# A two-layer decoder step: the third feed-forward layer's gate and up as Strassen products, and the state-space preparation moved beside the second

## Chip, core and metric

The kernel runs on one core of one Trainium2 chip. The metric is the device time of one execution in microseconds. PE is TensorE (matrix products), DVE is VectorE, ACT is ScalarE, POOL is GpSimd, and SP is the engine that issues most loads.

## What is computed

Two decoder layers run on 512 prompt tokens and 8 sample tokens, which the kernel keeps together as 520 columns. Each layer has a gated feed-forward layer, a mixer, a cross-attention and a second gated feed-forward layer. The mixer is a gated MLP in layer 0 and a diagonal state-space model in layer 1:

```python
def _swiglu(h, wg, wu, wd):
    return (jax.nn.silu(h @ wg) * (h @ wu)) @ wd
...
    for i in range(DEPTH):
        x = x + 0.5 * _swiglu(_rmsnorm(x, norm_ffn1[i]), ffn1_wg[i], ffn1_wu[i], ffn1_wd[i])
        ...
        x = x + out                                # mixer
        x = x + _cross_attn(...)
        x = x + 0.5 * _swiglu(_rmsnorm(x, norm_ffn2[i]), ffn2_wg[i], ffn2_wu[i], ffn2_wd[i])
    return _rmsnorm(x, norm_final), ...
```

The width is 1024, the hidden width 2816, everything in float32. So there are four feed-forward layers in time order: "first" (layer 0, before the mixer), "second" (layer 0, after it), "third" (layer 1, before the mixer) and "fourth". The state-space mixer needs tables made from its weights alone (powers of the diagonal times B and C, a convolution kernel, cosines and sines). This is the preparation that the change moves; it depends on nothing that the trunk computes.

## The kernel before

Activations lie transposed: 8 tiles of 128 features by 520 columns, in two halves of 260. A float32 product is made of three matmuls of rounded parts: weight-high times x-high, weight-high times x-low, weight-low times x-high. `wsplit` makes the parts: ACT rounds the raw weight `wr` into `wh` (line 121), and DVE, or POOL for every fourth weight (`pool_every`), subtracts to give `wl` (line 124). Each of `wr`, `wh` and `wl` has four buffers, and PSUM four tiles.

`ffn` (line 407) runs blocks of 256 hidden columns, 11 in all. `gu(j)` makes gate and up of one block with four calls of `lin`, 48 matmuls of 128x128 by 260 columns each, so 192. `down(a, b)` then takes hidden tiles a to b (128 columns each) through the down projection: 8 output tiles with 6(b−a) matmuls each, and DVE adds each output tile to X (lines 524 and 292 make the residual and the next layer's scaled input `xs`). Which hidden tiles go together is set by `FFN_GROUPS = ((0,6),(6,12),(12,18),(18,22))`. One `gu` beyond the group is always made ahead of its `down`, since line 558 runs `gu` up to `g1 // 2 + 1`.

The fourth layer has `seven=True`. Its first two blocks (`PLAIN = 2`) are plain; blocks 2 to 10 go through `gu7`, which makes each 2x2 block product (two halves of the inner dimension, 128-column halves of the weights, column halves of x) with seven products of 24 matmuls in place of eight, so 168. The price is sums: of x halves once per layer (`seven_x`, `xb` and `xt`, line 309), of weight quarters per block on POOL (`seven_begin`, line 348) and DVE, and of PSUM results on DVE. It uses `SEVEN_GROUPS`, in steps of four hidden tiles and a last one of two.

The state-space preparation `s5_prep` (line 1056) is a generator. `fill()` at the end of each `gu` and of each `down` but the last takes one more step of it. Before, the second and third layers both carry steps, and the rest is drained behind the third. In it POOL makes the powers in 128x128 pieces (`cmul`, lines 1214 to 1226), POOL and DVE make the phases (lines 1254 to 1264), PE turns and multiplies small tiles (line 80), and DVE copies them out (lines 1272 to 1293).

A layer's norm is applied late. DVE sums the squares of X (lines 235 and 236, POOL part of them), PE multiplies the sum with ones (`ones,sq`), DVE takes the inverse root, and the scale `rs` multiplies the first PSUM results. A scheduler places each engine's instructions in one fixed order when the program is built, and each engine runs its row in order.

Of the kernel before, what the change touches and what calls it, by code (L numbers as in the profile page):

```python
# [42 lines left out]
class Prog:  # L43
# [362 lines left out]

    def ffn(self, l, pre, fill=lambda: None, start=False, finish=None, seven=False):
        nc, ins = self.nc, self.ins
# [38 lines left out]
        def gu(j):  # L447
# [14 lines left out]
            for m in range(2):  # L462
# [15 lines left out]
                self.split(s, w)  # L478
                hid[2 * j + m] = s
            fill()  # L480

# [74 lines left out]
        done = 0  # L556
        for g0, g1 in SEVEN_GROUPS if seven else FFN_GROUPS:
            while done < min(DFF // 256, g1 // 2 + 1):
                (gu7 if seven and done >= PLAIN else gu)(done)
                done += 1  # L560
                if seven and done == 1:
                    ops, more = self.seven_x(key, xs)
                    late.append(more)
            if g1 == DFF // 128 and finish:
                last(g0, g1)
            else:
                down(g0, g1)
# [488 lines left out]
    def s5_prep(self):  # L1056
# [67 lines left out]
        nc.scalar.activation(s2, r, AF.Sin, scale=TP / 2)  # L1124
        pw = self.const([128, 5, 2, NPAIR], "pw")
        self.pw = pw
# [3 lines left out]
        V.tensor_sub(nr, em1, t)  # L1130
        V.tensor_scalar(pw[:, 1, 0], nr, 1.0, None, op0=ALU.add)
        V.tensor_mul(pw[:, 1, 1], mag, s1)
        ni = pw[:, 1, 1]
        den, a, b = f(), f(), f()
# [12 lines left out]
        V.tensor_mul(fim, a, den)  # L1147
        for j in range(2, 5):
            V.tensor_mul(a, pw[:, j - 1, 0], pw[:, 1, 0])
            V.tensor_mul(b, pw[:, j - 1, 1], pw[:, 1, 1])  # L1150
            V.tensor_sub(pw[:, j, 0], a, b)
            V.tensor_mul(a, pw[:, j - 1, 0], pw[:, 1, 1])
            V.tensor_mul(b, pw[:, j - 1, 1], pw[:, 1, 0])
            V.tensor_add(pw[:, j, 1], a, b)
# [51 lines left out]
        self.s5d = []  # L1206
        HQ = 8
        for hf in range(4):
            q0 = hf * HQ
            yield  # L1210
            MB, ME = (self.slot([128, 2, HQ, 4, 16], F32, "M") for _ in range(2))
            MB, ME = ([x[:, c] for c in range(2)] for x in (MB, ME))

            def cmul(dst, src, j, neg):
                ar, ai = bc16(pw[:, j, 0], q0, q0 + HQ), bc16(pw[:, j, 1], q0, q0 + HQ)
                xr, xi = src[:, 0, q0 : q0 + HQ], src[:, 1, q0 : q0 + HQ]
                a, b = (self.tmp([128, HQ, 16], tag="t") for _ in range(2))
                G.tensor_mul(a, xr, ar)
                G.tensor_mul(b, xi, ai)
                G.tensor_sub(dst[0], a, b)  # L1220
                a, b = (self.tmp([128, HQ, 16], tag="t") for _ in range(2))
                G.tensor_mul(a, xr, ai)
                G.tensor_mul(b, xi, ar)
                G.tensor_add(dst[1], a, b)
                if neg:
                    G.tensor_scalar(dst[1], dst[1], -1.0, None, op0=ALU.mult)

            for tau in range(4):
                if tau == 3:
                    for c in range(2):  # L1230
                        G.tensor_copy(MB[c][:, :, 3], Bb[:, c, q0 : q0 + HQ])
                else:
                    cmul([MB[c][:, :, tau] for c in range(2)], Bb, 3 - tau, False)
                cmul([ME[c][:, :, tau] for c in range(2)], CT, tau + 1, True)
            for i in range(2 * hf, 2 * hf + 2):
# [7 lines left out]
                for c in range(2):  # L1243
                    for g in range(2):
                        hp = slice(64 * g, 64 * g + 64)
                        nc.scalar.copy(Bs[hp, c, :, :, g], MB[c][hp, l0 : l0 + 4])
                        nc.scalar.copy(Es[hp, c, :, :, g], ME[c][hp, l0 : l0 + 4])
                        nc.scalar.activation(Cm[hp, c, :, g], CT[hp, c, 4 * i : 4 * i + 4], AF.Copy,
                                             scale=-1.0 if c else 1.0)
# [45 lines left out]
                for n, src, w in (("bi", bi, 1024), ("es", Es, 1024), ("tb", tb, 1024), ("tt", Tt, 512)):  # L1295
# [4 lines left out]
                    dd.append(d)  # L1300
                self.s5d.append(dd)

    def s5(self, fill=lambda: None):
# [85 lines left out]
        def emit(i, vv, H):  # L1389
# [4 lines left out]
            for t in range(4):  # L1394
                for j, (w, m) in enumerate(((Tt, vv), (Es[:, 0], H[0]), (Es[:, 1], H[1]))):
                    for a in range(4):
                        self.mm(p[32 * a : 32 * a + 32, t // 2, (t % 2) * 136 : (t % 2) * 136 + 136],
                                w[:, a, 32 * t : 32 * t + 32], m[:, a, 0:136], j == 0, j == 2)
            z = self.tmp()
# [22 lines left out]
        for i in range(KT):  # L1422
# [12 lines left out]
            prev = vv, H  # L1435
        ab = [self.pw[:, 1, c].unsqueeze(2).to_broadcast([128, NPAIR, NB]) for c in range(2)]
        h1 = []
# [122 lines left out]
    def run(self):  # L1560
# [7 lines left out]
        def drain(gen):  # L1568
            for _ in gen:
                pass  # L1570
# [11 lines left out]
        prep = self.s5_prep()  # L1582
        self.ffn(0, False, steps(prep))
        self.tap("ffn2_0")
        self.ffn(1, True, steps(prep))
        drain(prep)
        self.tap("ffn1_1")
# [36 lines left out]
```

## Time and profile before

| | us |
|---|---|
| median of 3 runs | 2456.07 |
| lowest, highest run | 2452.64, 2461.69 |
| the profiled execution's own time | 2454.6 |
| its span (first to last instruction) | 2452.9 |

The page names PE as the busiest engine, with 97% of the span. The windows view gives for a stretch the busy time of each engine, the clock that PE was granted (1.00 is the level of 2.4 GHz, 0.50 that of 1.2 GHz) and the load of the DMA engines. The timeline gives one row per instruction or run of equal instructions: start, duration, engine, line, operation, and in brackets the idle time ahead of it and who ended it. In the stretch from 912 to 1703 us stand the second layer (to 1306) and the third; the state-space mixer begins at about 1703 us and the fourth layer at 2072 us.

### The profile page before, as it was taken

How to read it: one execution, taken by the hardware profiler on the slowest of the kernel's cores; microseconds unless marked ns; L12 is line 12 of the kernel's file. 1: busy time of each engine (PE TensorE's matmuls, PEld its weight loads, DVE VectorE, ACT ScalarE, POOL GpSimd, SP SyncE). 2: the span in 40 equal slices, each digit the busy share in tenths (PEclk: the TensorE clock that was granted, in tenths of full speed). 3: DMA queues.
4: the chain of work that ended last, by engine and by line, in shares of the span. 5: the costliest groups of instructions: out<-in, count | busy, mean ns of one | idle time of the engine just before them, and what ended most of it. 6: DMA issues, size and time to landing. Idle time of an engine off the chain costs nothing. (4 is left out here: it accounts for less than half of the span.)

```text
span 2452.9 us, 46675 instructions
## 1 busy us (share of the span) xinstructions
PE 2386.8 (97%) x19943; PEld 2312.7 (94%) x19943; DVE 1456.5 (59%) x2500; ACT 849.0 (35%) x1312; POOL 526.5 (21%) x511
## 2 busy tenths in 40 slices
PE   8999999999999999999999999999989999999998
PEld 7999999999999789999999999998769979999998
DVE  6534343648556646545557555545993564788885
ACT  4323222432323333233234323323423333544443
POOL 2101111102112011262522625211040101122221
PEclk8999999999999999999999999999999999999998
DMA  6243433322224632324234343323752562133331
GB/s 191 86 139 108 151 97 94 113 88 62 87 87 160 226 130 79 117 79 142 82 117 134 100 134 104 121 87 129 265 183 92 174 228 98 52 104 93 98 104 53
DMA packets 235662, 293.34 MB, mean 120 GB/s; under 512 B 7423, under 2 KB 203767, under 8 KB 235455
## 3 DMA queue, kind: packets, MB, share of 16 engines
q1 hardware_dynamic: 222247, 254.88, 32.2%
q10 hardware_dynamic: 12567, 34.38, 4.0%
q8 instruction: 157, 2.57, 0.4%
q0 software_dynamic: 640, 1.10, 0.2%
q14 instruction: 51, 0.41, 0.1%
HBM read 264.77 MB, written 25.56 MB: 118 GB/s over the span
## 5 line engine op out<-in xcount | busy, mean ns | idle before, releaser
L77 PE MATMUL ps<-xs,wh 128*128 128x260 f32 x6592 | 1082.7, 284 | 3.9 <-ACT xs L291 2.5
L77 PEld LDWEIGHTS ps<-xs,wh 128*128 128x128 f32 x6592 | 918.6, 189 | 7.9 <-ACT xs L291 3.0
L77 PE MATMUL ps<-xs,wl 128*128 128x260 f32 x3296 | 689.4, 283 | 0.3 <-POOL wl L124 0.3
L121 ACT ACTIVATE wh<-wr 128x1024 fp32r<-128x1024 f32 (+2 forms) x388 | 353.5, 913 | 940.0 <-PE ps L77 846.1
L77 PEld LDWEIGHTS ps<-xs,wl 128*128 128x128 f32 x3296 | 520.7, 189 | 0.6 <-POOL wl L124 0.6
L124 POOL TENSOR_TENSOR wl<-wr,wh 128x1024 fp32r<-128x1024 f32 (+2 forms) x94 | 196.5, 2091 | 1349.1 <-ACT wh L121 1334.0
L77 PE MATMUL ps<-hid,wh 128*128 128x260 f32 (+1 forms) x2816 | 456.0, 283 | 2.8 <-ACT hid L161 1.8
L77 PEld LDWEIGHTS ps<-hid,wh 128*128 128x128 f32 x2816 | 388.4, 189 | 4.7 <-ACT hid L161 2.3
L124 DVE TENSOR_TENSOR wl<-wr,wh 128x1024 fp32r<-128x1024 f32 (+2 forms) x294 | 326.8, 1113 | 84.3 <-ACT wh L121 83.5
L77 PE MATMUL ps<-hid,wl 128*128 128x260 f32 (+2 forms) x1408 | 286.3, 283 | 0.0
L77 PEld LDWEIGHTS ps<-hid,wl 128*128 128x128 f32 x1408 | 218.2, 189 | 0.0
L524 DVE SCALAR_TENSOR_TENSOR X<-ps,X 128x520 f32<-128x520 f32 x136 | 94.7, 696 | 179.9 <-PE ps L77 179.6
L475 DVE TENSOR_TENSOR t<-ps,rs 128x520 f32<-128x520 f32 x70 | 48.8, 697 | 183.5 <-PE ps L77 182.5
L473 DVE TENSOR_TENSOR t<-ps,rs 128x520 f32<-128x520 f32 x70 | 48.8, 697 | 137.9 <-PE ps L77 105.6
L162 DVE TENSOR_TENSOR hid<-t,hid 128x520 fp32r<-128x520 f32 x88 | 87.1, 990 | 27.5 <-ACT hid L161 26.5
L161 ACT ACTIVATE hid<-t 128x520 fp32r<-128x520 f32 x88 | 56.2, 638 | 114.9 <-DVE t L476 110.2
L77 PE MATMUL ps<-o,wh 128*128 128x260 f32 x512 | 92.5, 291 | 1.2 <-DVE o L162 0.7
L77 PE MATMUL ps<-z,wh 128*128 128x260 f32 x512 | 83.3, 284 | 1.9 <-ACT t L1402 1.0
L77 PE MATMUL ps<-um,wh 128*128 128x260 f32 x512 | 82.5, 283 | 0.0
L77 PE MATMUL ps<-xt,wh 128*128 128x260 f32 x432 | 79.9, 285 | 1.6 <-ACT wh L344 1.6
L77 PEld LDWEIGHTS ps<-o,wh 128*128 128x128 f32 x512 | 74.5, 188 | 6.5 <-issue 3.0
L235 POOL TENSOR_TENSOR sq<-sq,sq 128x520 f32<-128x520 f32 x22 | 32.8, 1492 | 217.4 <-ACT sq L231 216.8
(352 smaller groups left out, 2946.0 us busy)
## 6 DMA issues: line engine op xcount, KB each, us to landing
wr<-in_ffn_wg SPq DMA_DIRECT2D x34, 1024.0 KB, 5.4
wr<-in_ffn_wu SPq DMA_DIRECT2D x34, 1024.0 KB, 5.4
wr<-in_ffn_wd SPq DMA_DIRECT2D x36, 768.0 KB, 4.7
wr<-in_ffn_wd SPq DMA_DIRECT2D x32, 512.0 KB, 3.5
wr<-in_a_w_in SPq DMA_DIRECT2D x16, 1024.0 KB, 5.5
kc<-in_cache_mem_k SPq DMA_DIRECT2D x32, 512.0 KB, 7.4
vc<-in_cache_mem_v SPq DMA_DIRECT2D x32, 512.0 KB, 7.6
wr<-in_ffn_wg SPq DMA_DIRECT2D x20, 512.0 KB, 3.9
```

What stands on the lines that cost most here:

```text
L77: self.nc.tensor.matmul(out, lhsT=lhsT, rhs=rhs, start=start, stop=stop, **kw)
L121: nc.scalar.activation(hi, r, AF.Copy)
L124: eng.tensor_sub(lo, r, hi.bitcast(F32))
L161: nc.scalar.activation(sl[:, 0, n0:n1], src, AF.Copy)
L162: nc.vector.tensor_sub(sl[:, 1, n0:n1], src, sl.bitcast(F32)[:, 0, n0:n1])
L235: (nc.gpsimd if k == 7 and early or k < 4 and not early else nc.vector).tensor_add(sums[-1], sums[-1], t)
L473: nc.vector.tensor_mul(self.v2(t), pg[:, :, :HN], rs)
L475: nc.vector.tensor_mul(self.v2(w), pu[:, :, :HN], rs)
L524: nc.vector.scalar_tensor_tensor(xv, p[:, :, :HN], 0.5, xv, op0=ALU.mult, op1=ALU.add)
```

## The change

The third layer is called with `seven=True` and without `fill`. The second layer is called with `fine=True`: it keeps the plain `gu`, takes two steps of the preparation in each `gu` instead of one, and uses `SEVEN_GROUPS`. While it runs `pool_every` is so large that no weight is split on POOL, and the preparation is drained at its end. `cmul` becomes `powers`, which makes three or four powers in one instruction on POOL (384 or 512 elements a row); a sign moves into ACT's copy (line 1246 of the kernel after), and the mixer reads the `es` table in the reversed order of powers.

```diff
-    def ffn(self, l, pre, fill=lambda: None, start=False, finish=None, seven=False):
+    def ffn(self, l, pre, fill=lambda: None, start=False, finish=None, seven=False, fine=False):
...
                 hid[2 * j + m] = s
+                if fine and m == 0:
+                    fill()
             fill()
...
-        for g0, g1 in SEVEN_GROUPS if seven else FFN_GROUPS:
+        for g0, g1 in SEVEN_GROUPS if seven or fine else FFN_GROUPS:
...
+        def powers(src, q0, i0):
+
+            M = self.slot([128, 2, HQ, 4, 16], F32, "M")
+            n = 4 - i0
+            sh = [128, HQ, n, 16]
+            ar, ai = (pw[:, i0:4, c, q0 : q0 + HQ].rearrange("p t q -> p q t").unsqueeze(3).to_broadcast(sh)
+                      for c in range(2))
+            xr, xi = (src[:, c, q0 : q0 + HQ].unsqueeze(2).to_broadcast(sh) for c in range(2))
+            for c, (x, y, op) in enumerate(((xr, xi, G.tensor_sub), (xi, xr, G.tensor_add))):
+                a, b = (self.tmp(sh, tag="t") for _ in range(2))
+                G.tensor_mul(a, x, ar)
+                G.tensor_mul(b, y, ai)
+                op(M[:, c, :, 0:n], a, b)
+            if n < 4:
+                G.tensor_copy(M[:, :, :, 3], src[:, :, q0 : q0 + HQ])
+            return M
+
+        nextB, nextE = powers(Bb, 0, 1), None
+        yield
+        nextE = powers(CT, 0, 0)
         for hf in range(4):
             q0 = hf * HQ
-            yield
-            MB, ME = (self.slot([128, 2, HQ, 4, 16], F32, "M") for _ in range(2))
...
+            MB, ME = ([x[:, c] for c in range(2)] for x in (nextB, nextE))
...
-                        nc.scalar.copy(Es[hp, c, :, :, g], ME[c][hp, l0 : l0 + 4])
+                        nc.scalar.activation(Es[hp, c, :, :, g], ME[c][hp, l0 : l0 + 4], AF.Copy,
+                                             scale=-1.0 if c else 1.0)
...
+                if hf < 3:
+                    if i % 2 == 0:
+                        nextB = powers(Bb, q0 + HQ, 1)
+                    else:
+                        yield
+                        nextE = powers(CT, q0 + HQ, 0)
...
         prep = self.s5_prep()
-        self.ffn(0, False, steps(prep))
+        self.pool_every = 1 << 30
+        self.ffn(0, False, steps(prep), fine=True)
+        drain(prep)
+        self.pool_every = 4
         self.tap("ffn2_0")
-        self.ffn(1, True, steps(prep))
-        drain(prep)
+        self.ffn(1, True, seven=True)
```

From the state-space mixer on, and before the second layer, the rows of all engines stay as they were. Three places in between follow.

The first is PE's row where the second layer ends and the third begins; `hid` is a hidden tile in the down projection, `xs` the scaled input of the next layer. Before:

```order
L77 MATMUL ps_14015<-hid_13779,wl_14008 128x260 x2
L77 MATMUL ps_14041<-hid_13011,wh_14011 128x260 x4
L77 MATMUL ps_14041<-hid_13011,wl_14012 128x260 x2
L77 MATMUL ps_14041<-hid_13118,wh_14011 128x260 x4
L77 MATMUL ps_14041<-hid_13118,wl_14012 128x260 x2
L77 MATMUL ps_14041<-hid_13672,wh_14011 128x260 x4
L77 MATMUL ps_14041<-hid_13672,wl_14012 128x260 x2
L77 MATMUL ps_14041<-hid_13779,wh_14011 128x260 x4
L77 MATMUL ps_14041<-hid_13779,wl_14012 128x260 x2
L77 MATMUL ps_14134<-xs_14067,wh_14116 128x260 x4
L77 MATMUL ps_14134<-xs_14067,wl_14117 128x260 x2
```

After:

```order
L77 MATMUL ps_14441<-hid_14090,wl_14424 128x260 x2
L77 MATMUL ps_14465<-hid_13937,wh_14457 128x260 x4
L77 MATMUL ps_14465<-hid_13937,wl_14458 128x260 x2
L77 MATMUL ps_14465<-hid_14090,wh_14457 128x260 x4
L77 MATMUL ps_14465<-hid_14090,wl_14458 128x260 x2
L77 MATMUL ps_14479<-hid_13937,wh_14461 128x260 x4
L77 MATMUL ps_14479<-hid_13937,wl_14462 128x260 x2
L77 MATMUL ps_14479<-hid_14090,wh_14461 128x260 x4
L77 MATMUL ps_14479<-hid_14090,wl_14462 128x260 x2
L77 MATMUL ps_14560<-xs_14493,wh_14542 128x260 x4
L77 MATMUL ps_14560<-xs_14493,wl_14543 128x260 x2
```

An output tile of the last `down` took four hidden tiles, with 24 matmuls; now it takes two, with 12.

The second is DVE's row at the same place, up to the last sum of squares (L236); L524 and L526 are the same residual sum, L292 the scaled input, L124 the weight split. Before:

```order
L292 SCALAR_TENSOR_TENSOR xs_14071<-X,gains,xs_14071 128x520
L292 SCALAR_TENSOR_TENSOR xs_14072<-X,gains,xs_14072 128x520
L235 TENSOR_TENSOR sq_14102<-sq_14102,sq_14104 128x520
L524 SCALAR_TENSOR_TENSOR X<-ps_14015,X 128x520
L124 TENSOR_TENSOR wl_14121<-wr_14114,wh_14120 128x1024
L292 SCALAR_TENSOR_TENSOR xs_14073<-X,gains,xs_14073 128x520
L235 TENSOR_TENSOR sq_14102<-sq_14102,sq_14107 128x520
L524 SCALAR_TENSOR_TENSOR X<-ps_14041,X 128x520
L124 TENSOR_TENSOR wl_14127<-wr_14124,wh_14126 128x1024
L292 SCALAR_TENSOR_TENSOR xs_14074<-X,gains,xs_14074 128x520
L235 TENSOR_TENSOR sq_14102<-sq_14102,sq_14110 128x520
L236 TENSOR_TENSOR sq_14091<-sq_14091,sq_14102 128x520
```

After:

```order
L526 SCALAR_TENSOR_TENSOR X<-ps_14479,X 128x520
L292 SCALAR_TENSOR_TENSOR xs_14497<-X,gains,xs_14497 128x520
L292 SCALAR_TENSOR_TENSOR xs_14498<-X,gains,xs_14498 128x520
L292 SCALAR_TENSOR_TENSOR xs_14499<-X,gains,xs_14499 128x520
L292 SCALAR_TENSOR_TENSOR xs_14500<-X,gains,xs_14500 128x520
L235 TENSOR_TENSOR sq_14528<-sq_14528,sq_14530 128x520
L124 TENSOR_TENSOR wl_14547<-wr_14540,wh_14546 128x1024
L235 TENSOR_TENSOR sq_14528<-sq_14528,sq_14533 128x520
L124 TENSOR_TENSOR wl_14553<-wr_14550,wh_14552 128x1024
L235 TENSOR_TENSOR sq_14528<-sq_14528,sq_14536 128x520
L124 TENSOR_TENSOR wl_14847<-wr_14844,wh_14846 128x1024
L236 TENSOR_TENSOR sq_14517<-sq_14517,sq_14528 128x520
```

Residual sums (X) alternated with the sums of squares; now the last residual sum comes eleven rows ahead of L236, and a third weight split (the next block's, wl_14847) stands among them.

The third is POOL's row inside the second layer, at the powers (`t` times `pw`, then `M`). Before:

```order
L124 TENSOR_TENSOR wl_10965<-wr_10958,wh_10964 128x768
L124 TENSOR_TENSOR wl_11068<-wr_11061,wh_11067 128x1024
L1218 TENSOR_TENSOR t_11287<-Bb_10685,pw 128x128
L1219 TENSOR_TENSOR t_11288<-Bb_10685,pw 128x128
L1222 TENSOR_TENSOR t_11292<-Bb_10685,pw 128x128
L1223 TENSOR_TENSOR t_11293<-Bb_10685,pw 128x128
L1218 TENSOR_TENSOR t_11297<-CT_10411,pw 128x128
L1219 TENSOR_TENSOR t_11298<-CT_10411,pw 128x128
L1222 TENSOR_TENSOR t_11302<-CT_10411,pw 128x128
L1223 TENSOR_TENSOR t_11303<-CT_10411,pw 128x128
L1218 TENSOR_TENSOR t_11308<-Bb_10685,pw 128x128
L124 TENSOR_TENSOR wl_11380<-wr_11373,wh_11379 128x1024
```

After:

```order
L1262 TENSOR_TENSOR t_10763<-t_10763,t_10775 128x512
L1225 COPY M_10954<-Bb_10217 128x16x16
L1221 TENSOR_TENSOR t_10955<-Bb_10217,pw 128x384
L1222 TENSOR_TENSOR t_10956<-Bb_10217,pw 128x384
L1221 TENSOR_TENSOR t_10960<-Bb_10217,pw 128x384
L1223 TENSOR_TENSOR M_10954<-t_10955,t_10956 128x8x48
L1222 TENSOR_TENSOR t_10961<-Bb_10217,pw 128x384
L1223 TENSOR_TENSOR M_10954<-t_10960,t_10961 128x8x48
L1241 MEMSET t_11075 128x256
L1254 TENSOR_SCALAR t_11092<-t_9941,w4h 128x128 x4
L1256 TENSOR_TENSOR t_11092<-t_11092,t_11093 128x512
```

The many pieces of 128x128, with weight splits among them, became few of 128x384 and 128x512, with no weight split among them.

## Rows read from the trace of the kernel before

**Rows 1.** Page: busy us, share of span, instructions, by engine.

```profile
PE 2386.8 (97%) x19943; PEld 2312.7 (94%) x19943; DVE 1456.5 (59%) x2500; ACT 849.0 (35%) x1312; POOL 526.5 (21%) x511
```

**Rows 2.** Windows: span, PE, PEld, DVE, ACT, POOL busy, PE clock, DMA share, GB/s.

```profile
912.00:1306.00 394.00, 389.92 (x3281) 387.45 (x3280) 222.69 (x383) 129.65 (x197) 139.11 (x170) 1.00 0.33 107
1306.00:1703.00 397.00, 392.11 (x3305) 388.79 (x3305) 211.80 (x321) 124.62 (x192) 125.49 (x162) 1.00 0.34 111
2072.00:2435.00 363.00, 359.03 (x2958) 358.31 (x2957) 287.35 (x366) 152.85 (x226) 74.34 (x36) 0.99 0.26 83
1606.00:1656.00 50.00, 50.00 (x419) 50.00 (x418) 20.20 (x23) 11.23 (x15) 3.68 (x2) 1.00 0.24 75
1356.00:1406.00 50.00, 50.00 (x429) 49.63 (x428) 27.55 (x31) 18.49 (x31) 33.30 (x51) 1.00 0.27 90
2207.00:2270.00 63.00, 63.00 (x530) 63.00 (x529) 52.66 (x62) 26.24 (x36) 14.09 (x6) 1.00 0.32 100
```

**Rows 3.** Timeline, PE: start, duration, work; one plain block's bounds, two product blocks' bounds.

```profile
1655.96 0.64 PE L77 MATMUL ps<-xs,wh 128*128 128x260 f32 x4
...
1679.02 0.63 PE L77 MATMUL ps<-hid,wh 128*128 128x260 f32 x4
...
2230.10 0.40 PE L77 MATMUL ps<-xs,wh 128*128 128x260 f32 x2
...
2270.34 0.64 PE L77 MATMUL ps<-hid,wh 128*128 128x260 f32 x4
```

**Rows 4.** Timeline, PE: first product block, fourth layer [idle before, its releaser].

```profile
2124.36 0.51 PE L77 MATMUL ps<-xt,wh 128*128 128x260 f32 x2 [1.64 <-ACT wh L344]
2125.31 0.78 PE L77 MATMUL ps<-xs,wh 128*128 128x260 f32 x2 [0.44 <-ACT wh L344]
```

**Rows 5.** Windows: after that start; then after the wait at the state-space mixer.

```profile
2126.00:2144.00 18.00, 18.00 (x142) 18.00 (x141) 14.00 (x19) 6.42 (x10) 0.00 (x0) 0.92 0.27 85
1712.00:1722.00 10.00, 10.00 (x37) 7.95 (x38) 7.33 (x26) 3.79 (x6) 0.26 (x2) 0.81 0.40 135
```

**Rows 6.** PE's waits, second and third layer: us in total, times, longest.

```profile
PE ps L80 <- DVE t L1279: 5.2, 6, 1.2
PE ps L77 <- ACT hid L161: 1.8, 2, 1.0
PE ps L77 <- DVE hid L162: 0.9, 1, 0.9
```

**Rows 7.** Timeline, PE: sums of squares, third layer and state-space mixer.

```profile
1312.57 1.25 PE L77 MATMUL ps<-ones,sq 128*128 128x1 f32 x10 [0.76 <-DVE sq L236]
...
1710.14 2.26 PE L77 MATMUL ps<-ones,sq 128*128 128x1 f32 x10 [5.01 <-DVE sq L236]
```

**Rows 8.** Timeline, DVE: around the start of the third layer.

```profile
1292.56 0.69 DVE L124 TENSOR_TENSOR wl<-wr,wh 128x512 fp32r<-128x512 f32 x1
...
1303.58 0.69 DVE L524 SCALAR_TENSOR_TENSOR X<-ps,X 128x520 f32<-128x520 f32 x1
...
1304.19 1.21 DVE L124 TENSOR_TENSOR wl<-wr,wh 128x1024 fp32r<-128x1024 f32 x1
...
1305.34 0.76 DVE L292 SCALAR_TENSOR_TENSOR xs<-X,gains,xs 128x520 fp32r<-128x520 f32 x1
...
1306.01 0.69 DVE L235 TENSOR_TENSOR sq<-sq,sq 128x520 f32<-128x520 f32 x1
...
1307.23 3.11 DVE L124 TENSOR_TENSOR wl<-wr,wh 128x1024 fp32r<-128x1024 f32 x1
```

**Rows 9.** Timeline, POOL: the split beside the last of these.

```profile
1306.86 2.40 POOL L124 TENSOR_TENSOR wl<-wr,wh 128x1024 fp32r<-128x1024 f32 x1 [7.06 <-ACT wh L121]
```

**Rows 10.** Groups, POOL, second and third layer: count, busy us, mean ns, idle before.

```profile
L124 POOL TENSOR_TENSOR wl<-wr,wh 128x1024 fp32r<-128x1024 f32 (+2 forms) x38 | 83.9, 2207 | 443.6 <-ACT wh L121 428.4 <-PE ps L80 15.1
...
L1220 POOL TENSOR_TENSOR M<-t,t 128x128 f32<-128x128 f32 x28 | 14.8, 528 | 0.0
...
L1256 POOL TENSOR_TENSOR t<-t,t 128x512 f32<-128x512 f32 x8 | 12.3, 1533 | 2.9 <-DVE t L1255 2.9
```

More of the change, by code (lines that the diff above doesn't have):

```diff
@@ L1124, in s5_prep @@
         nc.scalar.activation(s2, r, AF.Sin, scale=TP / 2)
-        pw = self.const([128, 5, 2, NPAIR], "pw")
+        pw = self.const([128, 4, 2, NPAIR], "pw")
         self.pw = pw
@@ L1130, in s5_prep @@
         V.tensor_sub(nr, em1, t)
-        V.tensor_scalar(pw[:, 1, 0], nr, 1.0, None, op0=ALU.add)
-        V.tensor_mul(pw[:, 1, 1], mag, s1)
-        ni = pw[:, 1, 1]
+        V.tensor_scalar(pw[:, 3, 0], nr, 1.0, None, op0=ALU.add)
+        V.tensor_mul(pw[:, 3, 1], mag, s1)
+        ni = pw[:, 3, 1]
         den, a, b = f(), f(), f()
@@ L1147, in s5_prep @@
         V.tensor_mul(fim, a, den)
-        for j in range(2, 5):
-            V.tensor_mul(a, pw[:, j - 1, 0], pw[:, 1, 0])
-            V.tensor_mul(b, pw[:, j - 1, 1], pw[:, 1, 1])
+        for j in (2, 1, 0):
+            V.tensor_mul(a, pw[:, j + 1, 0], pw[:, 3, 0])
+            V.tensor_mul(b, pw[:, j + 1, 1], pw[:, 3, 1])
             V.tensor_sub(pw[:, j, 0], a, b)
-            V.tensor_mul(a, pw[:, j - 1, 0], pw[:, 1, 1])
-            V.tensor_mul(b, pw[:, j - 1, 1], pw[:, 1, 0])
+            V.tensor_mul(a, pw[:, j + 1, 0], pw[:, 3, 1])
+            V.tensor_mul(b, pw[:, j + 1, 1], pw[:, 3, 0])
             V.tensor_add(pw[:, j, 1], a, b)
@@ L1207, in s5_prep @@
         HQ = 8
+        def powers(src, q0, i0):
[16 more added lines that the diff above has]
+        nextE = powers(CT, 0, 0)
         for hf in range(4):
             q0 = hf * HQ
-            yield
-            MB, ME = (self.slot([128, 2, HQ, 4, 16], F32, "M") for _ in range(2))
[L1212 to L1234, printed above, removed]
+            MB, ME = ([x[:, c] for c in range(2)] for x in (nextB, nextE))
             for i in range(2 * hf, 2 * hf + 2):
@@ L1397, in emit @@
                         self.mm(p[32 * a : 32 * a + 32, t // 2, (t % 2) * 136 : (t % 2) * 136 + 136],
-                                w[:, a, 32 * t : 32 * t + 32], m[:, a, 0:136], j == 0, j == 2)
+                                w[:, a, 32 * t : 32 * t + 32] if j == 0 else w[:, a, 96 - 32 * t : 128 - 32 * t],
+                                m[:, a, 0:136], j == 0, j == 2)
             z = self.tmp()
@@ L1435, in s5 @@
             prev = vv, H
-        ab = [self.pw[:, 1, c].unsqueeze(2).to_broadcast([128, NPAIR, NB]) for c in range(2)]
+        ab = [self.pw[:, 3, c].unsqueeze(2).to_broadcast([128, NPAIR, NB]) for c in range(2)]
         h1 = []
```

## Prediction

> **What bounds the kernel now.** I read the page's first part, then the windows, then PE's timeline and waits, DVE's timeline at the layer boundaries, and POOL's groups. PE is busy for 97% of the span [rows 1]. By windows it is busy 389.9 of 394 us in the second layer and 392.1 of 397 in the third, at the full clock, while DVE has 223 and 212, POOL 139 and 125, and the DMA engines a third [rows 2]. So PE decides both layers: fewer matmuls shorten them, and everything else counts only where it makes PE wait. The fourth layer, which has the products already, is the nearest thing to what the third becomes: DVE is there at 287 of 363 us, and in its dense part at 52.66 of 63, with PE at 63.00 of 63 [rows 2].
>
> **Products in the third layer.** A plain block of 192 matmuls lasts from 1655.96 to 1679.02, 23.06 us; two product blocks last from 2230.10 to 2270.34, 40.24, so 20.12 each [rows 3]. That is 0.120 us per matmul in both, so the 24 matmuls saved are worth 2.9 us as PE stays fed. Nine blocks change: 9 x 2.9 = −26.1.
>
> The first product block has a ramp. In the fourth layer PE waits 1.64 and 0.44 us there for ACT's rounded weights, 2.1 together [rows 4], and the clock then stands at 0.92 over 18 busy us [rows 5], a loss of 0.08 x 18 = 1.4. The third layer gets the same instructions in the same order: +3.5. Bounds: +2 if the clock holds, +5 if POOL, which has to make the weight sums, is late; in the dense window it is busy 14 of 63 us [rows 2].
>
> The second layer's and the third's waits for a hidden tile, 1.8 and 0.9 us [rows 6], come from a `down` that needs the tile just made. With groups of four the last block is followed by the `down` of hidden tiles 16 to 20, which were ready long before: −2.7 (bounds −2.7 and 0).
>
> **The start of the third layer.** This is the new wait that I see. PE needs the sum of squares after the first `lin`; before it waited 0.76 us for it [rows 7]. The last `down` of the second layer now has 12 matmuls per output tile, 12 x 0.120 = 1.44 us, 11.5 for the eight; before it was 23. In these, DVE owes 8 residual sums at 0.69, 8 scaled inputs at 0.76, 4 splits of 1024 at 1.21, 4 sums of squares at 0.69 (L235 three times, L236 once) [rows 8], and 4 splits of 256, estimated from the 1024 and 512 rows (1.21 and 0.69) at 0.43: 5.5 + 6.1 + 4.8 + 2.8 + 1.7 = 20.9 us. The first residual sum can't start before 1.44, so the last sum ends 22.3 us after the `down` begins, 10.8 behind its end. Two of the small splits can be done ahead (−0.9); a 1024 split beside one on POOL took 3.11 [rows 8, 9], 1.9 more. So 10 to 12.7. The first `lin`, 48 matmuls, covers 48 x 0.120 = 5.8. PE waits 4.2 to 6.9; I take 5.5, which is +4.7 against the 0.76. Behind the wait stand only PE's later matmuls, and behind the sums on DVE the rest of the norm, which PE doesn't reach earlier.
>
> After such a wait the clock falls: behind the 5.01 us at the state-space mixer [rows 7] it stood at 0.81 over 10 busy us [rows 5], where 0.19 x 10 = 1.9 were lost. I add 1.3 (0 to 1.9). Sum: +6 (bounds +3 and +9).
>
> At the end of the third layer the same small `down` stands ahead of the mixer, whose wait is 5.01 us already. There too the `down` gets shorter, but its DVE work has no preparation among it any more. By the same count the sum of squares ends about 5.6 us behind the last matmul, and 1.5 us of other work on PE stands ahead of it: about 4.2. That is −0.8 (−2 to +1.5).
>
> **The preparation in the second layer.** It asks for 25 steps; 22 half blocks and 5 `down`s give 27, so nothing is left to drain. PE's matmuls in it are the same ones; they move from the third layer into the second. Its waits at the transposes, 5.2 us in six [rows 6], come from a copy on DVE between two short pieces of PE work; in the new order the same copies stand with less PE work between them at one place and more at another. I take 0 (−4 if most vanish, +4 if all eight units wait as long as the longest, 8 x 1.2 = 9.6 less 5.2).
>
> DVE there: in a stretch without preparation, 1606 to 1656, it is busy 20.20 of 50 us [rows 2], 0.40, so 159 of 394. All of the preparation's DVE work is what the two windows have above that share, 64 + 52 = 116. The splits that leave POOL are 19 of the 38 [rows 10], at about 1.1 each 21, and 16 more residual sums at 0.69 are 11. Together 307 of some 400 us, 77%, below the 84% that the fourth layer's dense part carries with PE never idle [rows 2]. So this costs little: +1 (0 to +8, if bursts of it delay a weight split beyond the four buffers' cover; 8 is one split's time in each step of the eight units).
>
> POOL has the splits no more, so what stands behind a late piece of the preparation on its row is only more preparation. Its loads in POOL's queue stay at the front of the second layer. The tables' stores go from ACT's queue as before, only earlier; ACT is at 130 of 394 us [rows 2]. More and smaller loads of the down weights move the same bytes, at a DMA share of a third [rows 2]. I count these at nothing.
>
> **Sum.** −26.1 + 3.5 − 2.7 + 6 − 0.8 + 0 + 1 = −19.1. The profiled execution took 2454.6 in its own time, so 2435.5. The median of the runs, 2456.07, is 1.5 above it: 2437.
>
> **Rivals.**
>
> *DVE and POOL exclude each other.* The 3.11 us split ran from 1307.23 to 1310.34, and POOL's ended at 1309.26 [rows 8, 9]; from there 1.08 us remain, as much as the split takes alone. So DVE may have stood still meanwhile. If every microsecond of POOL's work did that, the second layer needs DVE's 307 plus POOL's preparation. Of POOL's 265 us in both layers [rows 2] 84 are splits [rows 10] and some 9 sums of squares; of the 172 left, some 190 pieces at 0.528 (100) become 52 wider ones, at most 1.53 each [rows 10] and on the way of their widths rather 1.2 (62). So about 130. 307 + 130 = 437 against some 400: the layer is bound by DVE and costs 37 more, 60 if DVE can be filled to 95% only. That gives 2474 to 2497, slower than before; I name 2480. It decides from the point where the two together exceed the layer. Before they made 223 + 139 = 362 of 394 [rows 2], so nothing there speaks against it. Against it: from 1356 to 1406 they were busy 60.9 us in 50 while PE was never idle [rows 2].
>
> The Trainium skill, "SBUF — State Buffer", section "SBUF: two separate sides", calls the port pair that DVE and GpSimd share an exclusive lock, which a DVE operation with two inputs in SBUF takes against a GpSimd operation that reads SBUF, and "the other fully blocks". The split's row agrees with it, the window of 60.9 us shows that it can't hold for all of DVE's work, and by the rule in full the time would be the rival's.
>
> *Most of the gain is eaten.* Start of the third layer at +9, transposes at +4, bursts at +8, ramp at +5, hidden-tile waits as now: 3 + 4 + 7 + 1.5 + 2.7 = 18 above the sum, 2455; at three quarters of it 2451. For it: each is a wait that DVE ends, and DVE gets denser in both layers. Against: PE doesn't wait at DVE's 84% in the fourth layer.
>
> *No new wait.* If DVE clears the boundary in time, or the clock holds: 2437 − 6 = 2431, and with fewer waits at the transposes 2427. Against it stands the count of 20.9 us.
>
> That the change doesn't do what it says I exclude: the matmuls are 216 fewer in PE's row.
>
> **Chances.** Forecast (2431 to 2444) 0.62, no new wait (below 2431) 0.14, gain mostly eaten (2444 to 2456) 0.16, exclusion 0.08, of which 0.03 stays below 2468, if only a part of POOL's work stops DVE. A measurement of this kernel can tell about 0.5%, 12.3 us, from no change: faster is below 2443.8, slower above 2468.4. Faster 0.76, same 0.19, slower 0.05. The range 2428 to 2451 leaves out some 0.06 below and 0.13 above.
>
> **What would show it.** Right: blocks of the third layer at 20.1 us, two waits for ACT's `wh` at its third block, a wait of 4 to 7 us for the sum of squares at its start with a lower clock behind it, and PE full in the second layer. Wrong: PE waiting for DVE's `wl` or hidden tiles all through the second layer, DVE there above 350 us, or preparation work behind the second layer's last `down`.

## The result and the profile after

The changed kernel takes 2436.78 us (median of 4 runs, 2435.37 to 2439.48), the kernel before 2456.8; the ratio is 0.9922, 95% interval 0.9906 to 0.9939. Six further runs have a median of 2438.91, ratio 0.9928 (0.9913 to 0.9943). The profiled execution took 2439.48 with a span of 2437.8; before it was 2454.6 and 2452.9. So the profiled execution gained 15.1 us and the medians 18 to 20.

The page's first part after: PE has the same share and fewer matmuls, DVE is busier.

```profile
PE 2368.4 (97%) x19727; PEld 2295.6 (94%) x19727; DVE 1600.0 (66%) x2707; ACT 902.6 (37%) x1421; POOL 482.1 (20%) x365
```

The windows view, columns as in [rows 2]: two long stretches, cut at 1310, and four short ones. The cut at 1310 lies inside the last `down` of the second layer. By PE's timeline the second layer runs from 912.19 to 1316.91, 404.7 us, where it was 393.9 (911.76 to 1305.70): it now holds all of the preparation's matmuls. The third runs to 1685.69, 368.8 us, where it was 397.5 (to 1703.22). In the first 398 us of the second layer's stretch DVE is busy for 281.

```profile
912.00:1310.00 398.00, 393.54 (x3349) 389.21 (x3349) 281.06 (x526) 144.26 (x253) 141.33 (x140) 1.00 0.37 119
1310.00:1692.00 382.00, 370.22 (x3041) 369.02 (x3040) 306.08 (x395) 168.81 (x253) 88.09 (x50) 0.98 0.33 104
979.00:984.00 5.00, 4.62 (x26) 4.62 (x27) 4.08 (x5) 0.64 (x1) 4.10 (x5) 0.66 0.22 54
1328.00:1345.00 17.00, 16.50 (x111) 16.41 (x112) 7.22 (x23) 2.99 (x5) 2.56 (x1) 0.80 0.36 114
1380.00:1398.00 18.00, 18.00 (x142) 18.00 (x141) 14.12 (x19) 6.59 (x10) 0.00 (x0) 0.93 0.32 102
1693.00:1703.00 10.00, 10.00 (x34) 8.23 (x35) 6.59 (x24) 2.96 (x5) 0.25 (x2) 0.65 0.59 209
```

The third layer's product blocks, from the start of two to the start of the next `down` (timeline of PE): 40.30 us, so 20.15 each, as in [rows 3].

```profile
1421.06 0.41 PE L77 MATMUL ps<-xs,wh 128*128 128x260 f32 x2
...
1461.36 0.40 PE L77 MATMUL ps<-hid,wh 128*128 128x260 f32 x2
```

PE's waits in both layers (us in total, times, longest). Those at the transpositions and for hidden tiles [rows 6] are gone, but for 0.36 us at the transpositions, in pieces too small for the view. Three in the second layer are new (`hb`, `t L475`, `CT`: 4.0 us), as are the ramp and a second long wait for the sum of squares.

```profile
PE ps L77 <- DVE sq L236: 9.6, 2, 5.0
PE ps L77 <- ACT wh L344: 2.1, 2, 1.6
PE ps L80 <- DVE hb L1206: 2.0, 1, 2.0
PE ps L77 <- DVE t L475: 1.6, 1, 1.6
PE ps L77 <- DVE CT L1183: 0.4, 1, 0.4
PE ps L77 <- DVE xs L292: 0.3, 1, 0.3
```

The two long ones in PE's timeline: the third layer's start, 5.04 us where it was 0.76, and the mixer's, 4.53 where it was 5.01 [rows 7].

```profile
1328.50 1.84 PE L77 MATMUL ps<-ones,sq 128*128 128x1 f32 x8 [5.04 <-DVE sq L236]
...
1692.12 1.20 PE L77 MATMUL ps<-ones,sq 128*128 128x1 f32 x5 [4.53 <-DVE sq L236]
```

The clock behind the waits stands in the windows above: 0.80 over 17 us from 1328, behind the third layer's start; 0.65 over 10 us at the mixer, where it was 0.81 [rows 5]; 0.93 in the ramp; and 0.66 over 5 us from 979, behind the new waits of the second layer.

**The new waits in the second layer.** Their cause is in DVE's timeline ahead of them. The last piece of the set-up of the powers is a chain of 18 small operations of 128x32. Most take 0.19 us, but six in a row, from 959.09 on, take 0.98 to 1.34 each, and two later ones 0.76. Behind them on DVE's row stands L475, which empties the PSUM tile that PE needs; it starts at 968.58, and PE stood from 967.8 to 969.4.

```profile
958.86 0.19 DVE L1151 TENSOR_TENSOR t<-pw 128x32 f32<-128x32 f32 x1
959.09 0.98 DVE L1153 TENSOR_TENSOR pw<-t,t 128x32 f32<-128x32 f32 x1
960.10 0.99 DVE L1154 TENSOR_TENSOR t<-pw 128x32 f32<-128x32 f32 x1
961.01 1.09 DVE L1155 TENSOR_TENSOR t<-pw 128x32 f32<-128x32 f32 x1
962.14 0.98 DVE L1156 TENSOR_TENSOR pw<-t,t 128x32 f32<-128x32 f32 x1
...
964.30 1.34 DVE L1152 TENSOR_TENSOR t<-pw 128x32 f32<-128x32 f32 x1
...
968.47 0.19 DVE L1156 TENSOR_TENSOR pw<-t,t 128x32 f32<-128x32 f32 x1
968.58 0.69 DVE L475 TENSOR_TENSOR t<-ps,rs 128x520 f32<-128x520 f32 x1
```

POOL's timeline beside it: products of 128x512, one a microsecond. DVE's slow operations end where POOL's do (960.07, 961.09, 962.10 against POOL's 960.02, 961.04, 962.06).

```profile
958.96 1.06 POOL L1188 TENSOR_TENSOR t<-bn,fim 128x512 f32<-128x512 f32 x1 [9.59 <-DVE t L1152]
959.98 1.06 POOL L1192 TENSOR_TENSOR t<-bn,fim 128x512 f32<-128x512 f32 x1
961.00 1.06 POOL L1187 TENSOR_TENSOR Bb<-bn,fre 128x512 f32<-128x512 f32 x1
962.02 1.06 POOL L1190 TENSOR_TENSOR Bb<-bn,fre 128x512 f32<-128x512 f32 x1
```

### The profile page after: what moved, and what is told of

It reads as the page before. It is cut to its first block, busy times and chain, and to the rows that moved or that the text cites. A ratio compares the mean times of both kernels' runs of the same rounds, so it can differ in the third digit from the quotient of the medians.

```text
span 2437.8 us, 46575 instructions
## 1 busy us (share of the span) xinstructions
PE 2368.4 (97%) x19727; PEld 2295.6 (94%) x19727; DVE 1600.0 (66%) x2707; ACT 902.6 (37%) x1421; POOL 482.1 (20%) x365
## 5 line engine op out<-in xcount | busy, mean ns | idle before, releaser
L77 PE MATMUL ps<-xs,wh 128*128 128x260 f32 x6016 | 1006.9, 285 | 6.6 <-ACT xs L291 2.4
L77 PEld LDWEIGHTS ps<-xs,wh 128*128 128x128 f32 x6016 | 854.4, 190 | 11.8 <-issue 3.2
L121 ACT ACTIVATE wh<-wr 128x1024 fp32r<-128x1024 f32 (+3 forms) x384 | 322.1, 840 | 815.5 <-PE ps L77 750.5
L124 DVE TENSOR_TENSOR wl<-wr,wh 128x1024 fp32r<-128x1024 f32 (+3 forms) x314 | 324.1, 1033 | 78.7 <-ACT wh L121 72.1
L124 POOL TENSOR_TENSOR wl<-wr,wh 128x1024 fp32r<-128x1024 f32 (+3 forms) x70 | 136.6, 1953 | 1142.4 <-ACT wh L121 1142.4
L526 DVE SCALAR_TENSOR_TENSOR X<-ps,X 128x520 f32<-128x520 f32 x168 | 116.9, 697 | 143.9 <-PE ps L77 143.5
L77 PE MATMUL ps<-xt,wh 128*128 128x260 f32 x864 | 158.8, 284 | 3.3 <-ACT wh L344 3.3
L77 PEld LDWEIGHTS ps<-xt,wh 128*128 128x128 f32 x864 | 134.5, 190 | 3.7 <-ACT wh L344 3.7
L77 PE MATMUL ps<-xt,wl 128*128 128x260 f32 x432 | 123.1, 285 | 0.0
L475 DVE TENSOR_TENSOR t<-ps,rs 128x520 f32<-128x520 f32 x52 | 36.3, 698 | 126.4 <-PE ps L77 126.4
L344 ACT ACTIVATE wh<-S 128x1024 fp32r<-128x1024 f32 x72 | 75.3, 1060 | 90.9 <-PE ps L77 86.5
L345 DVE TENSOR_TENSOR wl<-S,wh 128x1024 fp32r<-128x1024 f32 x72 | 100.3, 1402 | 12.3 <-ACT wh L344 12.2
```

Source lines behind the costliest of these rows:

```text
L77: self.nc.tensor.matmul(out, lhsT=lhsT, rhs=rhs, start=start, stop=stop, **kw)
L121: nc.scalar.activation(hi, r, AF.Copy)
L124: eng.tensor_sub(lo, r, hi.bitcast(F32))
L344: self.nc.scalar.activation(hi, src, AF.Copy)
L345: self.nc.vector.tensor_sub(lo, src, hi.bitcast(F32))
L475: nc.vector.tensor_mul(self.v2(w), pu[:, :, :HN], rs)
```

## Experiments

Each is an edit of the changed kernel. Ratios are to the kernel before on the same chip, with 95% intervals. The changed kernel itself stood among them:

> The changed kernel as it is, beside the next three. Theory 1 (the forecast's sum is right for the usual run, the profiled one was late in parts that the change doesn't touch): median within 1.5 us of 2437. Rival (the profiled run is the usual one, the terms of the sum are 4 us too small): median 2439 to 2441.

2438.91 us, 0.9928 (0.9913 to 0.9943). The two theories are 2 us apart and the two medians, 2436.78 and 2438.91, stand on either side: undecided, though a second profile shows the same waits at the same places.

**Groups of six in the second layer (second_groups6).**

```diff
-        for g0, g1 in SEVEN_GROUPS if seven or fine else FFN_GROUPS:
+        for g0, g1 in SEVEN_GROUPS if seven else FFN_GROUPS:
```

> The changed kernel, but the second layer's down projection keeps the old groups of six hidden tiles and a last one of four. Theory 1 (the short last group leaves too little PE time for DVE's norm work): the wait for the sum of squares at the third layer's start falls from 5.0 us to about 1, the lower clock behind it goes, and one or two waits for hidden tiles, 1.8 us together, come back; 4 to 6 us less than the changed kernel. Rival (DVE is late there because its whole second layer is denser now): the wait stays above 3.5 us and the time within 2 us of the changed kernel.

2437.51 us, 0.9926 (0.9913 to 0.9939): no change. The wait at the third layer's start did fall, from 5.04 to 0.38, as theory 1 has it (4.5 of the 4.9 below are the mixer's). But the transpositions, which wait 0.36 us in all in the changed kernel, now wait 9.7 us. PE's waits:

```profile
PE ps L80 <- DVE t L1279: 9.7, 5, 2.7
PE ps L77 <- DVE sq L236: 4.9, 2, 4.5
```

So the short last `down` is what makes the start wait; what the groups of six give back there they take at the transpositions, since the same steps then fall beside other work; that last reading was not tested by itself.

**Half steps from the third block on (late_halfsteps).**

```diff
-                if fine and m == 0:
+                if fine and m == 0 and j > 1:
```

> The changed kernel, but the extra half steps of the preparation begin only in the third block of the second layer, so its first two steps lie a whole block apart. Theory 1 (near 959 to 968 us the chain of small DVE operations was held up by POOL's products beside it, and with it the read of PSUM queued behind): chain and products no longer lie side by side, the chain's operations take about 0.2 us instead of 1, PE's 4.1 us of waits there and the 1.7 us of lower clock go; 5 to 6 us less. Rival 1 (dense steps as such hold DVE up): the same waits appear two blocks later, time within 2 us of the changed kernel. Rival 2: the later end of the preparation reaches into the last down projection and costs what it gains.

2437.35 us, 0.9925 (0.9911 to 0.9939): no change, and theory 1's premise was not met. POOL's products wait for the factor `fim`, which DVE makes just ahead of the chain; however far apart the steps are, the two begin together. The wait for L475, 1.6 us at 968 in the changed kernel, is now 3.4 us at 988. The preparation now ends inside the last `down`, and a weight split of the third layer came 6.7 us late (rivals 1 and 2 both hold). PE's waits:

```profile
PE ps L77 <- DVE wl L124: 6.7, 1, 6.7
PE ps L77 <- DVE sq L236: 4.5, 1, 4.5
PE ps L77 <- DVE t L475: 3.4, 1, 3.4
```

**Both, with a last group of six (both).** The edits of late_halfsteps (above) and of groups_4446 (below) together.

> The changed kernel with the late half steps, and with groups of 4, 4, 4, 4 and 6 hidden tiles in the second layer, so that its last down projection has 36 matmuls per output tile. Theory 1 (the two losses add and are independent): 9 to 12 us less than the changed kernel, about 2427; the last group of six needs its newest tiles only 2.9 us into an output tile, so under 1 us of waits for them. Rival (the end of the preparation or the hidden tiles wait instead): 3 to 6 us less.

2443.59 us, 0.9949 (0.9936 to 0.9963), 5 to 7 more than the changed kernel: neither. The preparation's end in the last `down` holds up the scaled inputs (4.1 us of waits) and the sum of squares (3.3 and 4.5).

**The chain ahead of the factors (chain_first).** The edit moves the loop that makes the powers up, behind the allocation of `den`.

```diff
         den, a, b = f(), f(), f()
+        for j in (2, 1, 0):
+            V.tensor_mul(a, pw[:, j + 1, 0], pw[:, 3, 0])
+            ...
         V.tensor_mul(den, are, are)
...
         V.tensor_mul(fim, a, den)
-        for j in (2, 1, 0):
-            ...
```

> The changed kernel, with the chain of 18 small DVE operations (the powers) written ahead of the two factors that POOL's products wait for, so that they can't lie side by side. Theory 1 (DVE's small operations stood still while POOL's products ran): each takes about 0.2 us again instead of up to 1.3, DVE reads the waiting PSUM result some 6 us earlier, and PE's waits between 967 and 984 (4.1 us, and 1.7 of lower clock) shrink to under 2 us in all: 4 to 5 us less than the changed kernel, 2433 to 2434. Rival (these operations are slow by waiting for each other, or the turn of the tables behind them is late anyway): the operations stay near 1 us, or the wait only moves to the next read: within 2 us of the changed kernel.

2427.23 us, 0.9893 (0.9872 to 0.9913). The chain's operations take 0.19 us, L475 starts at 961.15 instead of 968.58, and all three new waits are gone. The five runs fall in two groups, 2426.5 to 2427.2 and 2432.3 to 2433.1, and the profiled one is in the second. DVE's timeline, chain's end, L475 and a split behind it:

```profile
959.58 0.19 DVE L1143 TENSOR_TENSOR pw<-t,t 128x32 f32<-128x32 f32 x1
...
961.04 0.19 DVE L1156 TENSOR_TENSOR fim<-t,t 128x32 f32<-128x32 f32 x1
961.15 0.69 DVE L475 TENSOR_TENSOR t<-ps,rs 128x520 f32<-128x520 f32 x1
...
962.91 2.08 DVE L124 TENSOR_TENSOR wl<-wr,wh 128x1024 fp32r<-128x1024 f32 x1
```

POOL's timeline beside the split:

```profile
961.37 1.06 POOL L1188 TENSOR_TENSOR t<-bn,fim 128x512 f32<-128x512 f32 x1 [12.60 <-DVE fim L1156]
...
963.87 2.04 POOL L1187 TENSOR_TENSOR Bb<-bn,fre 128x512 f32<-128x512 f32 x1
```

Theory 1 holds for the mechanism: POOL's product of 963.87 now takes 2.04 us instead of 1.06, and DVE's split beside it 2.08 instead of 1.21. The span is 7.2 us shorter than the changed kernel's, of which 6.1 lie in the second layer, where theory 1 has 4 to 5; the medians differ by 10 to 12, and the rest I can't assign.

**Groups 4, 4, 4, 4, 6 with the early steps (groups_4446).**

```diff
+FINE_GROUPS = ((0, 4), (4, 8), (8, 12), (12, 16), (16, 22))
...
-        for g0, g1 in SEVEN_GROUPS if seven or fine else FFN_GROUPS:
+        for g0, g1 in SEVEN_GROUPS if seven else FINE_GROUPS if fine else FFN_GROUPS:
```

> The changed kernel with its steps, but groups of 4, 4, 4, 4 and 6 hidden tiles in the second layer. Theory 1 (the wait at the third layer's start is the shortness of the last down projection; with the groups of six it was the transpositions' place that cost the gain, which stays as in the changed kernel up to the last group): the 5.0 us wait falls under 1.5 us, the waits at the transpositions stay under 1 us in all, 5 to 7 us less than the changed kernel. Rival (any regrouping shifts the built order so that waits of the same size appear elsewhere): within 2 us.

2425.84 us, 0.988 (0.986 to 0.990): 11 to 13 less than the changed kernel, twice what theory 1 has. The wait at the third layer's start and the lower clock behind it are gone, and the transpositions wait 0.34 us in all; from one sum of squares to the next the second layer is 5.9 us shorter, the third 2.7, the mixer 2.4. The 2.4 can't be put down to the edit: that stretch lies between 218.2 and 223.2 us in the traces of these runs whatever was changed, and in the next run, which has the same groups, it is as in the changed kernel. The first two, 8.6, are what the edit gains.

**Both of these (chain_4446).**

> Both of these edits together. If both theories hold and are independent: 9 to 12 us less than the changed kernel, about 2427. If either rival holds: about 2432, with the corresponding waits in the trace.

2423.49 us, 0.9873 (0.9855 to 0.9892). It is the fastest kernel here, 13 to 15 us below the changed one; its span is 2421.7. In the second layer the two edits add: 6.1 and 5.9 us alone, 11.9 together, from one sum of squares to the next. The medians don't (10 to 12 and 11 to 13 alone). PE's waits in both layers are the mixer's and the ramp:

```profile
PE ps L78 <- DVE sq L237: 4.5, 1, 4.5
PE ps L78 <- ACT wh L345: 2.1, 2, 1.6
```

**The third layer plain (third_plain).**

```diff
-        self.ffn(1, True, seven=True)
+        self.ffn(1, True)
```

> The changed kernel, but the third layer's gate and up stay plain (no products there), and the preparation is beside the second layer as in the change. Theory 1 (the forecast's sum): the nine blocks give back 26 us, the ramp (4 us) goes, so 22 us more than the changed kernel, about 2460, which is 3 to 4 above the kernel before: the move of the preparation by itself gains nothing and costs the wait at the third layer's start. Rival (the move by itself gains, since the third layer is rid of the preparation's waits and work on DVE and POOL): 2450 or less.

2458.76 us, 1.0024 (1.0011 to 1.0037): theory 1. The products are worth 20 to 22 us net of their ramp; the preparation's move without them costs about 4 to 6. (Without `seven` the third layer also goes back to groups of six, and the mixer's wait is then 6.5 us where it was 4.5, so the 20 to 22 include that.)

**Splits back on POOL in the second layer (second_pool4).** 

```diff
-        self.pool_every = 1 << 30
         self.ffn(0, False, steps(prep), fine=True)
         drain(prep)
-        self.pool_every = 4
```

> The changed kernel, but every fourth weight split of the second layer stays on POOL as before the change. Theory 1 (the splits' place was no matter, DVE has room at 75%): within 3 us of the changed kernel. Rival (POOL's preparation delays the splits queued behind it, and PE waits for them): waits for POOL's wl in the second layer, 5 to 20 us more.

2460.55 us, 1.0018 (1.0007 to 1.0030), 22 to 24 more than the changed kernel: the rival, and beyond its 20. PE's waits in the second layer:

```profile
PE ps L80 <- DVE t L1279: 12.8, 4, 3.8
PE ps L77 <- POOL wl L124: 5.1, 2, 4.9
PE ps L80 <- DMA t<-in_b_c_im: 3.4, 1, 3.4
```

POOL's row is in order, so a split and a piece of preparation hold each other up: 5.1 us for the splits directly, and 12.8 at the transpositions; DVE, which makes these ready, waits 17.6 and 14.1 us for POOL's phases there (L1254 and L1256). From one sum of squares to the next the second layer is 22.8 us longer. How much of it is the order of POOL's row, and how much that splits on POOL and DVE's work hold each other up, this run doesn't separate.

**Idle POOL work in the third layer (pool_mul, pool_set, pool_reads).** These measure the rival "DVE and POOL exclude each other". In each product block POOL gets 20 products of constants, or 50 memory sets, or 40 products that read the block's weight sum; nothing reads the results.

```diff
             begun[j] = self.seven_begin(*r)
+            for x in range(40 if pre else 0):
+                nc.gpsimd.tensor_mul(self.junk, begun[j][2][:, x % 2, x // 2 % 4], self.ident)
```

> The changed kernel with 20 idle products of 128x128 elements (a constant times a constant, into a tile that nobody reads) on POOL in each of the third layer's nine product blocks, some 8 to 10 us of POOL work per block of 20 us. DVE is busy there for about 84%. Theory 1 (POOL work that reads two operands holds DVE's two-operand work up, so that both together must fit the block): DVE's operations get longer, the blocks get longer than 20.1 us, and the time rises by 14 us (if half of DVE's work is hit) to 50 us (if all of it is). Rival (the two engines overlap freely in the main; the near second per operation seen at 959 us was a matter of small operations only): under 3 us more, blocks at 20.1 us.

> The same with 50 memory sets of the same tile in place of the 20 products, so POOL work of about the same length that reads nothing. Theory 1 (only POOL work that reads excludes DVE): within 3 us of the changed kernel, DVE's operations as they were. Rival (any POOL work does, or the weight sums behind it on POOL's row come late): 14 us or more, as with the products.

2474.16 us, 1.0079 (1.0063 to 1.0096), and 2447.69 us, 0.9972 (0.9959 to 0.9986). Neither tells anything of the third layer, whose length did not change (363.6 and 362.0 us from one sum of squares to the next, 363.6 and 363.7 in the changed kernel's two traces): having no input from the blocks, the work was placed at the program's start and delayed POOL's first weight splits there. They gave one number: such a product takes 0.46 us (median of 180).

> The changed kernel with 40 idle products of 128x128 on POOL in each of the third layer's nine product blocks, each reading a part of the block's first weight sum, so that they stay beside their block (in the earlier try they read constants alone and stood at the program's start). Alone such a product takes about 0.21 us, so 8.6 us in a block of 20.1; the order of PE and DVE is that of the changed kernel. Theory 1 (POOL work with two operands holds DVE's work up, and the two together must fit the block): DVE's weight splits become clearly longer than 1.42 us, the blocks longer than 20.1 us, the time 10 to 50 us more. Rival (DVE keeps its pace and POOL is the one that yields): POOL's products take well over 0.21 us each, DVE's operations keep their length within a tenth, blocks stay at 20.1 us and the time rises by at most a few us, where a weight sum behind such products comes late.

2515.39 us, 1.0261 (1.0231 to 1.0290): 77 to 79 more than the changed kernel, beyond both. The 0.21 us in the expectation was my error; the run before has 0.46, so 40 products are 18 us. POOL's window and its products in the dense stretch (columns as in [rows 2] and [rows 10]):

```profile
1400.00:1700.00 300.00, 247.16 (x1917) 244.26 (x1916) 195.41 (x217) 90.08 (x124) 241.69 (x313) 0.91 0.25 78
```

```profile
L502 POOL TENSOR_TENSOR junk<-S,ident 128x128 f32<-128x128 f32 x290 | 193.8, 668 | 21.9
```

Some of DVE's groups in the same stretch of that kernel; all but L529, which reads PSUM, have two operands from SBUF:

```profile
L346 DVE TENSOR_TENSOR wl<-S,wh 128x1024 fp32r<-128x1024 f32 x28 | 39.9, 1425 | 32.1 <-ACT wh L345 32.1
L346 DVE TENSOR_TENSOR wl<-wr,wh 128x1024 fp32r<-128x1024 f32 x22 | 32.1, 1460 | 1.4 <-ACT wh L345 1.4
L529 DVE SCALAR_TENSOR_TENSOR X<-ps,X 128x520 f32<-128x520 f32 x32 | 22.3, 696 | 60.2 <-PE ps L77 60.2
...
L512 DVE TENSOR_TENSOR t<-t,rs 128x520 f32<-128x520 f32 x20 | 19.0, 951 | 0.3
L514 DVE TENSOR_TENSOR t<-t 128x260 f32<-128x260 f32 x26 | 14.9, 573 | 2.9 <-ACT t L513 2.9
```

and two of them in the changed kernel, 1400 to 1680:

```profile
L345 DVE TENSOR_TENSOR wl<-S,wh 128x1024 fp32r<-128x1024 f32 x32 | 45.3, 1424 | 5.8 <-ACT wh L344 5.8
...
L511 DVE TENSOR_TENSOR t<-t 128x260 f32<-128x260 f32 x33 | 14.0, 424 | 3.9 <-ACT t L510 3.9
```

DVE's splits keep their 1.42 and the 260-wide products grow by 35%, while the sums that read PSUM (L529) keep 0.70 (L524 takes 0.69 in [rows 8]). POOL's products have a mean of 0.67, but not because each got longer: half of the 290, those with no such DVE operation beside them, take 0.46, and the other half 0.88 on average. So both engines wait for each other, operation by operation, and neither theory has who yields.

The time went up as theory 1 has it, but more than these waits add to it. POOL's row is in order, and the idle products stand in it ahead of a split or a weight sum that PE needs. One such place, on POOL, PE and DVE in turn:

```profile
1499.77 9.96 POOL L502 TENSOR_TENSOR junk<-S,ident 128x128 f32<-128x128 f32 x14
1509.69 1.26 POOL L124 TENSOR_TENSOR wl<-wr,wh 128x512 fp32r<-128x512 f32 x1
1510.91 11.97 POOL L502 TENSOR_TENSOR junk<-S,ident 128x128 f32<-128x128 f32 x19
```

```profile
1511.00 0.80 PE L77 MATMUL ps<-hid,wl 128*128 128x260 f32 x2 [8.68 <-POOL wl L124]
```

```profile
1515.74 0.70 DVE L529 SCALAR_TENSOR_TENSOR X<-ps,X 128x520 f32<-128x520 f32 x1 [11.11 <-PE ps L77]
```

DVE stood idle for 11.11 us, so it held nobody up there; POOL's products followed each other every 0.53 us, and the split of 1509.69 stood behind 21 of them. These took 14.6 us from 1495.14 on; at 0.53 each they would have taken 11.1. So at this place most of the delay is the row's length and about 3.4 us is DVE's part. PE's waits in the layer are 34.7 us for POOL's splits, 8.6 to 8.8 each, and 19.4 for ACT's copies of PSUM (L384); at the one of these that I followed, at 1543, DVE's work ahead of them had begun late because POOL's sum stood behind 13 products. The two causes, the order of POOL's row and the shared time with DVE, are not separated over the layer.

## Why the prediction was right

The time and the sign were right, 2437 against 2436.78 to 2438.91; the exactness is partly luck, since terms of the sum were off in both directions: the 4.8 us that vanished at the transpositions and the 4.8 by which "DVE denser" exceeded its +1 cancel. Against the profiled execution, where the sum of −19.1 stood against −15.1:

| step | forecast | measured | where |
|---|---|---|---|
| nine product blocks | −26.1 | −26.2 | 20.15 us a block |
| ramp | +3.5 | +3.4 | waits of 2.1, clock 0.93 over 18 us |
| hidden-tile waits | −2.7 | −2.7 | none left |
| third layer's start | +6 | +7.7 | wait +4.3, clock 0.20 x 17 = 3.4 |
| mixer's start | −0.8 | +1.1 | wait −0.5, clock 0.65 for 0.81 over 10 us |
| transpositions | 0 | −4.8 | 0.36 us left |
| DVE denser | +1 | +5.8 | waits 4.1, clock 0.34 x 5 = 1.7 |

These make −15.7. The parts of the span that the change doesn't touch came out 1.8 us longer, and a remainder of 1.2 I leave unassigned.

**Blocks, ramp, start of the third layer** came as worked out. The wait there was counted at 4.2 to 6.9 us, taken as 5.5, and was 5.04; second_groups6 and groups_4446 show that the short `down` is its cause. Only the clock's loss behind it was mis-sized: 3.4 against 1.3, and outside the bound of 1.9, which came from a window of 10 us only. For the mixer's start the prediction gives 5.6 us without a working; the sum of squares ended 6.3 us behind the last product matmul, 1.9 us of other work on PE stood between, and the wait was 4.53 for the 4.2 named.

**The step that failed is "So this costs little: +1" together with "I take 0" for the transpositions.** I counted DVE's busy share, 307 of 400 us (281 of 398 in the trace), and had bursts only as a bound. The loss came from one burst in which DVE was not short of time but stood still for POOL, while a PSUM read was queued behind it. The split of 3.11 us [rows 8, 9] had shown that; I used it for a rival that sums whole engines, and not for the one place where many small operations meet POOL's long ones. chain_first shows the cause by taking the overlap away. The transpositions' waits I left at zero by argument; they vanished, and came back when the groups were changed (second_groups6), so they hang on what the steps lie beside.

**The rival of exclusion** (0.08) named a real mechanism with the wrong sum: not all of DVE's work shares the time with POOL's. Operations that read PSUM don't: L529 keeps 0.70 us in pool_reads, where two-operand work beside POOL grows (L512 0.95 for 0.69). In the changed kernel's second layer some 98 of DVE's 281 us read PSUM (L526, L473, L475 and the copies and sums of the preparation), so at most 183 + 141 = 324 of 398 us are left for the pair, and PE lost nothing to it but the one burst. The kernel before shows that a single operand from SBUF can be enough: L1255, 0.42 us otherwise, took 2.61 from 1383.84 on, beside a split on POOL of 2.40 from 1383.77 on. My argument against the rival, 60.9 us busy in 50 [rows 2], was no argument, since an operation that stands still counts as busy: 0.98 us for 0.19 of work in the chain. The Trainium skill, "SBUF — State Buffer", section "SBUF: two separate sides", has the operation that starts first hold the shared pair "for the whole instruction"; DVE's ends at POOL's ends agree. As the prediction quotes the rule, it names DVE operations with two inputs in SBUF, so even in full it doesn't give the rival's 307 us.

**What I counted at nothing** held in the changed kernel but hid a large choice: that POOL's row carries no splits in the second layer is worth 22 to 24 us (second_pool4). I had named the row's order as the reason and not priced it. What the wider instructions of `powers` are worth by themselves no run tests.

## What to carry to other kernels

A busy share says whether an engine has time, not whether it is there when it is needed: look at what stands behind a chain of small operations on its row, and what another engine runs beside them. A transfer of work that shortens the last stage of a layer takes away the cover of the next layer's norm; make the last group long, and see that nothing else ends inside it. Two regroupings that looked alike (6, 6, 6, 4 and 4, 4, 4, 4, 6) differed by 11 to 12 us, so such numbers want trying, with the waits of each read beside the time.

## What the runs showed of the hardware

A DVE operation of 128x32 with two operands in SBUF took 0.19 us alone. Beside POOL's products and sums of 128x512, with operands in SBUF too, it took 0.98 to 1.34, and each of the six ended within 0.05 us of the end of one of POOL's. In the other direction POOL's product of 128x512 took 2.04 instead of 1.06 us beside a DVE split. DVE's sums that read PSUM kept 0.70 us beside POOL's products. After a wait of 5.04 us PE's clock, at 0.80 over 17 us, cost 3.4 us more, two thirds of the wait again.
